# Scan states of an SSM block: float32 products become split float32r products, B·C work moves into the next product block, a modulation row is loaded earlier

## The chip, the cores and the metric

The kernel runs on one core of a Trainium2 chip. The metric is the device time of one execution in microseconds (us), shown as the median of several runs. A core has TensorE (PE, matrix products, with its weight loads shown apart as PEld), VectorE (DVE), ScalarE (ACT), GpSimd (POOL) and SyncE (SP), which here only issues transfers. Each engine works through its own queue in order and waits there for what an instruction needs.

## The reference

All is float32, with a sequence of S = 512 and a width of D = 2048. A first block (Mamba-2 like) is followed by a second one (RG-LRU and attention) whose input is scaled and shifted by a modulation `mod = silu(c) @ w_ada + b_ada`. The change touches the scan of the first block and the loading of c.

```python
proj = rmsnorm(x) @ w_in                       # z, x, B, C, dt
xbc = silu(conv4(x, B, C)); dt = softplus(dt + bias); a = -exp(a_log)
# per chunk of the sequence, 8 groups of 8 heads of 64:
cb = einsum(C, B); y_diag = einsum(cb, decay, x * dt)
y_off = einsum(C, state, exp(cs))
state = state * exp(cs_last) + einsum(B, exp(cs_last - cs), x * dt)
y = rmsnorm((y_diag + y_off + d_skip * x) * silu(z)) @ w_out
```

## The kernel before

Every large float32 product is made of three float32r products ("gemm"): each operand is split into a high half (float32r) and a low half (the rest), and weight-high times act-high, weight-high times act-low and weight-low times act-high are summed (lines 197 to 199). `wchunk` loads 512 KB of weights by SP into one of three `raw` buffers; ScalarE copies each half of it to `hi` (L171) and VectorE subtracts it to get `lo` (L172). `hi` and `lo` have three buffers each, so the split for a later chunk half waits until TensorE has read an earlier one.

The input projection is a loop over 8 groups g. A group is five product blocks of 96 products (16 k-tiles, two column halves, three products): B and C, then for each unit u = 0, 1 (four heads) an x block and a z block. Small steps are placed in a block at a k-tile by `mid[kt]`: `bc_late` (transposes btp of B, products cbp of C and B, the transposed B as btok, the masked cbm) at k-tile 11 of the x block of u = 0; in each z block `ssd_pre` at 11 (transposes tp of x; xdt and xdw, x times dt and times the weight of the state), `ssd_decay` at 12 (four tiles dec per unit, exponentials on ScalarE, then times cbm on VectorE; and cex) and `ssd_states` at 14 (sa, sb: the products of btok and xdw for three chunks; st: the running states). The first unit of the first group has these steps in the next x block. After the z block comes `ssd_unit`: 56 products into yp, chunk 3 first, from dec and xdt (L1186) and from cex and st (L1188). A scheduler writes each engine's order from the program and its priorities; `issue_after` and `high_priority` bind or favour an instruction.

Spread over the groups stand the 96 dot products of `ada` (VectorE, L1214), each on 512 KB of w_ada loaded into one of two buffers. The row c has two halves: when dot product 0 or 48 comes up, its half is loaded (L1205), put through tanh (ScalarE) and finished by two VectorE steps. Dot product 48 falls into group 4, u = 0.

## Time and profile before

| | |
|---|---|
| median of 3 runs | 2068.11 us (2066.47 to 2069.34) |
| profiled execution | 2072.64 us, its span in the trace 2070.9 us |
| PE busy | 2050.8 us (99%), 10032 products |
| PEld busy | 1700.3 us (82%) |
| DVE busy | 1314.9 us (63%) |
| ACT busy | 928.7 us (45%) |
| transfers | 277.26 MB, mean 134 GB/s |
| granted TensorE clock, mean | 0.996 |

The profile shows one execution, which took a little longer than the median of the runs; a sum made from its rows is compared with its own time. Busy time is the union of an engine's instructions. A TensorE row of the timeline says when a product began and how long it was in the engine; products overlap, so the distance of starts is what a product costs in a stream.

### The profile page before, as it was taken

Reading aid. Unit: us, or ns where it says so; the run is one execution under the profiler, and the core shown is the slowest. Engines: PE = TensorE matmul, PEld = TensorE weight load, DVE = VectorE, ACT = ScalarE, POOL = GpSimd, SP = SyncE. Lnnn points to the kernel's source line nnn. Section 1 sums busy time; section 2 is a strip of 40 time slices with the busy share of each in tenths; the row PEclk is TensorE's granted clock in tenths of the full one; section 3 lists DMA queues with packets and bytes.
Section 4 is the critical chain, followed back from the end, with each engine's and each line's share of the span. In section 5 each row is a group of like instructions: output and inputs, shape, how many; then the busy total and the mean of one; then the engine's idle time right before and its main releaser. Section 6 shows DMA issues by size and latency. Waiting matters only on the chain.

```text
span 2070.9 us, 26917 instructions
## 1 busy us (share of the span) xinstructions
PE 2050.8 (99%) x10032; PEld 1700.3 (82%) x10032; DVE 1314.9 (63%) x2308; ACT 928.7 (45%) x1744; POOL 45.4 (2%) x35
## 2 busy tenths in 40 slices
PE   8999999999999999999999999989999999999999
PEld 7888888888878888888788888868888888888887
DVE  6777777687777768777644545476666664764333
ACT  6473444444344443444432433344554554763222
POOL 0000000000000000000000000000000000000000
PEclk9999999999999999999999999989999999999999
DMA  6344555545455454444533332224222223233442
GB/s 227 114 153 159 179 176 187 166 152 182 154 184 170 170 173 147 163 163 135 181 122 128 107 99 95 82 93 159 77 69 67 67 66 105 85 112 106 149 142 92
DMA packets 92627, 277.26 MB, mean 134 GB/s; under 512 B 9744, under 2 KB 19984, under 8 KB 90448
## 3 DMA queue, kind: packets, MB, share of 16 engines
q1 hardware_dynamic: 92208, 275.54, 40.6%
q8 instruction: 78, 1.28, 0.2%
q14 instruction: 53, 0.43, 0.1%
q10 hardware_dynamic: 288, 0.01, 0.0%
HBM read 262.80 MB, written 12.71 MB: 133 GB/s over the span
## 4 chain that ended last, share of the span: by engine, by line
PE 94%; DVE 2%; DMA 1%; ACT 1%; issue 1%; DVEq 0%; ACTq 0%
PE g L197 26%; PE g L198 26%; PE g L199 26%; PE gt L266 1%; PE yp L1186 1%; PE gt L267 1%; PE gt L268 1%; PE yp L1188 1%; DMA adaw<-in_wada 1%; PE op L914 1%; PE g L217 1%; DVE lo L172 1%; PE g L219 1%; PE g L218 1%; PE fm L1060 1%
## 5 line engine op out<-in xcount | busy, mean ns | idle before, releaser
L172 DVE TENSOR_TENSOR lo<-raw,hi 128x512 fp32r<-128x512 f32 (+2 forms) x704 | 476.6, 677 | 544.4 <-ACT hi L171 542.3
L171 ACT ACTIVATE hi<-raw 128x512 fp32r<-128x512 f32 (+2 forms) x704 | 426.8, 607 | 868.6 <-PE g L198 780.8
L197 PE MATMUL g<-hn,hi 128*128 128x512 f32 x1216 | 480.0, 395 | 0.0
L199 PE MATMUL g<-hn,lo 128*128 128x512 f32 x1216 | 474.2, 390 | 0.0
L198 PE MATMUL g<-hn,hi 128*128 128x512 f32 x1216 | 473.9, 390 | 0.0
L197 PEld LDWEIGHTS g<-hn,hi 128*128 128x128 f32 x1216 | 228.3, 188 | 48.8 <-issue 2.4
L199 PEld LDWEIGHTS g<-hn,lo 128*128 128x128 f32 x1216 | 228.2, 188 | 47.8 <-issue 0.2
L198 PEld LDWEIGHTS g<-hn,hi 128*128 128x128 f32 x1216 | 228.4, 188 | 46.7 <-issue 0.2
L198 PE MATMUL g<-h,hi 128*128 128x512 f32 x512 | 200.4, 391 | 1.1 <-DVE h L689 0.8
L197 PE MATMUL g<-ya,hi 128*128 128x512 f32 x512 | 200.2, 391 | 0.0
L199 PE MATMUL g<-ya,lo 128*128 128x512 f32 x512 | 200.2, 391 | 0.0
L198 PE MATMUL g<-ya,hi 128*128 128x512 f32 x512 | 200.0, 391 | 0.0
L199 PE MATMUL g<-h,lo 128*128 128x512 f32 x512 | 199.9, 390 | 0.0
L197 PE MATMUL g<-h,hi 128*128 128x512 f32 x512 | 199.7, 393 | 0.0
L1214 DVE CUSTOM_DVE_ANT_0 adaw<-adaw,adac 128x1024 f32<-128x1024 f32 x96 | 115.6, 1221 | 21.8 <-DMA adaw<-in_wada 21.8
L198 PEld LDWEIGHTS g<-h,hi 128*128 128x128 f32 x512 | 96.2, 188 | 22.5 <-DVE h L689 3.2
L197 PEld LDWEIGHTS g<-ya,hi 128*128 128x128 f32 x512 | 96.5, 188 | 20.4 <-ACT st L1143 0.2
L198 PEld LDWEIGHTS g<-ya,hi 128*128 128x128 f32 x512 | 96.5, 189 | 20.2 <-issue 0.2
L199 PEld LDWEIGHTS g<-ya,lo 128*128 128x128 f32 x512 | 96.4, 188 | 20.3 <-DVE lo L172 0.4
L199 PEld LDWEIGHTS g<-h,lo 128*128 128x128 f32 x512 | 96.1, 188 | 20.3
L197 PEld LDWEIGHTS g<-h,hi 128*128 128x128 f32 x512 | 95.9, 188 | 20.1 <-ACT h L688 1.0
L337 DVE SCALAR_TENSOR_TENSOR xc<-pr,cwh,xc 128x511 f32<-128x511 f32 (+1 forms) x144 | 101.8, 746 | 0.0
(364 smaller groups left out, 2609.9 us busy)
## 6 DMA issues: line engine op xcount, KB each, us to landing
raw<-in_win SPq DMA_DIRECT2D x216, 512.0 KB, 3.5
adaw<-in_wada SPq DMA_DIRECT2D x96, 512.0 KB, 4.7
raw<-in_wout SPq DMA_DIRECT2D x88, 512.0 KB, 3.5
csr<-csd SPq DMA_DIRECT2D x16, 1024.0 KB, 4.8
xT<-in_xT SPq DMA_DIRECT2D x16, 256.0 KB, 4.3
raw<-in_win SPq DMA_DIRECT2D x16, 256.0 KB, 3.2
ydram<-y SPq DMA_DIRECT2D x16, 256.0 KB, 2.1
yst<-ydram SPq DMA_DIRECT2D x8, 512.0 KB, 4.4
```

The lines of the kernel that those rows point to most:

```text
L171: self.last_hi = nc.scalar.activation(hi, raw[:, i * h : i * h + h], AF.Copy).ins
L172: self.last_lo = nc.vector.tensor_tensor(lo, raw[:, i * h : i * h + h], hi.bitcast(F32), ALU.subtract).ins
L197: nc.tensor.matmul(ps[j], hi[:, c], a[:, 0, :], start=kt == 0, stop=False)
L198: nc.tensor.matmul(ps[j], hi[:, c], a[:, 1, :], start=False, stop=False)
L199: mm = nc.tensor.matmul(ps[j], lo[:, c], a[:, 0, :], start=False, stop=kt == nkt - 1)
L217: nc.tensor.matmul(ps[j], hi[:, o], a[:, 0, :], start=first, stop=False)
L218: nc.tensor.matmul(ps[j], hi[:, o], a[:, 1, :], start=False, stop=False)
L219: mm = nc.tensor.matmul(ps[j], lo[:, o], a[:, 0, :], start=False, stop=last)
L266: nc.tensor.matmul(ps[t], a[:, 0, ts], hi, start=k == 0, stop=False)
L267: nc.tensor.matmul(ps[t], a[:, 0, ts], lo, start=False, stop=False)
L337: nc.vector.scalar_tensor_tensor(xc[:, s:], ps[:, : S - s], w(k), xc[:, s:], ALU.mult, ALU.add)
L1214: nc.vector.tensor_tensor_reduce(out=raw, in0=raw, in1=self.cb, op0=ALU.mult, op1=ALU.add, scale=1.0, scalar=0.0, accum_out=self.macc[:, i ...
```

## The change

The state products take split operands: btok and xdw get a high half (ScalarE copy) and a low half (VectorE subtraction), with xw as the unsplit product, and each of the three chunks is three float32r products. The second state is formed straight from the first's PSUM, and the combining steps have high priority. `bc_late` moves to k-tile 11 of the z block of u = 0, ahead of `ssd_pre`, with PSUM tiles from the pool of yp; the steps of u = 1 come one k-tile earlier. The first products of the block that follows a unit are ordered behind the unit's last product (`fence`). The second half of c is loaded when dot product 47 is issued, and its tanh is ordered behind a weight split.

```diff
@@ -142,6 +142,7 @@
     def __init__(self, tc, I, O, dbg):
         self.tc, self.nc, self.I, self.O, self.dbg = tc, tc.nc, I, O, dbg
         self.n = 0
+        self.fence = None
 
     def nm(self, s):
         self.n += 1
@@ -191,13 +192,15 @@
                     after(kt)
                 a = acts[kt]
                 hi, lo = hl[k * 2 // nk]
-                for j in range(ncol):
-                    o = k % (nk // 2) * width + j * P
-                    c = slice(o, o + P)
-                    nc.tensor.matmul(ps[j], hi[:, c], a[:, 0, :], start=kt == 0, stop=False)
-                    nc.tensor.matmul(ps[j], hi[:, c], a[:, 1, :], start=False, stop=False)
-                    mm = nc.tensor.matmul(ps[j], lo[:, c], a[:, 0, :], start=False, stop=kt == nkt - 1)
-                    self.mms.append(mm.ins)
+                with self.tc.issue_after(self.fence) if self.fence is not None and kt == 0 else nullcontext():
+                    for j in range(ncol):
+                        o = k % (nk // 2) * width + j * P
+                        c = slice(o, o + P)
+                        nc.tensor.matmul(ps[j], hi[:, c], a[:, 0, :], start=kt == 0, stop=False)
+                        nc.tensor.matmul(ps[j], hi[:, c], a[:, 1, :], start=False, stop=False)
+                        mm = nc.tensor.matmul(ps[j], lo[:, c], a[:, 0, :], start=False, stop=kt == nkt - 1)
+                        self.mms.append(mm.ins)
+                self.fence = None
                 kt += 1
         assert kt == nkt
         return ps
@@ -507,15 +510,16 @@
             bt = self.conv_silu(ps[0], 32 + g, tmp.tile([P, S], F32, tag="B", name=f"B{g}", bufs=1), prs[0])
             ct = self.conv_silu(ps[1], 40 + g, tmp.tile([P, S], F32, tag="C", name=f"C{g}", bufs=1), prs[1])
             flush()
-            btok = tmp.tile([P, 3, P], F32, tag="btok", name=f"btok{g}", bufs=1)
+            btok = tmp.tile([P, 2, 3, P], F32R, tag="btok", name=f"btok{g}", bufs=1)
             cbm = tmp.tile([P, NC, P], F32, tag="cbm", name=f"cbm{g}", bufs=1)
 
             def bc_late(g=g, bt=bt, ct=ct, btok=btok, cbm=cbm):
-                btp = self.pa.tile([P, NC, P], F32, tag="a", name=f"btp{g}")
+                btp = self.py.tile([P, NC, P], F32, tag="y", name=f"btp{g}")
                 for c in range(3):
                     nc.tensor.transpose(btp[:, c, :], bt[:, c * P : c * P + P], self.ckc("ident"))
-                nc.scalar.activation(btok, btp[:, 0:3, :], AF.Copy)
-                cbp = self.pa.tile([P, NC, P], F32, tag="a", name=f"cbp{g}")
+                nc.scalar.activation(btok[:, 0], btp[:, 0:3, :], AF.Copy)
+                nc.vector.tensor_tensor(btok[:, 1], btp[:, 0:3, :], btok[:, 0].bitcast(F32), ALU.subtract)
+                cbp = self.py.tile([P, NC, P], F32, tag="y", name=f"cbp{g}")
                 for c in range(NC):
                     nc.tensor.matmul(cbp[:, c, :], bt[:, c * P : c * P + P], ct[:, c * P : c * P + P],
                                      start=True, stop=True)
@@ -525,7 +529,6 @@
 
             slow = None
             if g:
-                mid[11] = [bc_late]
                 self.ada(2)
             else:
                 mid[11] = [dt_late]
@@ -552,7 +555,8 @@
                          lambda g=g, u=u, btok=btok, pre=pre: self.ssd_states(g, u, btok, pre)]
                 unit = lambda g=g, u=u, xs=xs, pre=pre, yy=yg: self.ssd_unit(g, u, xs, pre, yy)
                 if g or u:
-                    mid.update({11: steps[0:1], 12: steps[1:2], 14: steps[2:3]})
+                    mid.update({10: steps[0:1], 11: steps[1:2], 13: steps[2:3]} if u else
+                               {11: [bc_late, steps[0]], 12: steps[1:2], 14: steps[2:3]})
                     late.append(unit)
                 else:
                     slow = {1: [bc_late], 5: steps[0:1], 6: steps[1:2], 9: steps[2:3]}
@@ -1108,7 +1112,7 @@
         csr = tmp.tile([P, 4, S], F32, tag="csr", name=self.nm("csr"), bufs=1)
         nc.sync.dma_start(csr, self.csd[h0 : h0 + 4, :].unsqueeze(0).to_broadcast([P, 4, S]))
         xdt = tmp.tile([P, NC, 4, 64], F32, tag="xdt", name=self.nm("xdt"), bufs=1)
-        xdw = tmp.tile([P, 3, 4, 64], F32, tag="xdw", name=self.nm("xdw"), bufs=1)
+        xdw = tmp.tile([P, 2, 3, 4, 64], F32R, tag="xdw", name=self.nm("xdw"), bufs=1)
         for c2 in range(2):
             tp = self.pa.tile([P, 2, 4, 64], F32, tag="a", name=self.nm("tp"))
             for c in range(2):
@@ -1120,9 +1124,12 @@
             nc.vector.tensor_tensor(xdt[:, a:b], tp,
                                     self.dt[:, a:b, h0 : h0 + 4].unsqueeze(3).to_broadcast([P, 2, 4, 64]), ALU.mult)
             b2 = min(b, 3)
-            nc.vector.tensor_tensor(xdw[:, a:b2], tp[:, 0 : b2 - a],
+            xw = tmp.tile([P, 2, 4, 64], F32, tag="xw", name=self.nm("xw"), bufs=1)[:, 0 : b2 - a]
+            nc.vector.tensor_tensor(xw, tp[:, 0 : b2 - a],
                                     self.dtw[:, a:b2, h0 : h0 + 4].unsqueeze(3).to_broadcast([P, b2 - a, 4, 64]),
                                     ALU.mult)
+            nc.scalar.activation(xdw[:, 0, a:b2], xw, AF.Copy)
+            nc.vector.tensor_tensor(xdw[:, 1, a:b2], xw, xdw[:, 0, a:b2].bitcast(F32), ALU.subtract)
         pre.update(csr=csr, xdt=xdt, xdw=xdw)
 
 
@@ -1134,17 +1141,20 @@
         sb = self.pa.tile([P, 1, 4, 64], F32, tag="a", name=self.nm("sb"))
         parts = [sa[:, 0], sa[:, 1], sb[:, 0]]
         for c in range(3):
-            nc.tensor.matmul(parts[c].rearrange("p h d -> p (h d)"), btok[:, c, :],
-                             xdw[:, c].rearrange("p h d -> p (h d)"), start=True, stop=True)
+            o = parts[c].rearrange("p h d -> p (h d)")
+            for i, (a, b) in enumerate(((0, 0), (0, 1), (1, 0))):
+                nc.tensor.matmul(o, btok[:, a, c, :], xdw[:, b, c].rearrange("p h d -> p (h d)"),
+                                 start=i == 0, stop=i == 2)
         st = []
         for c in range(3):
             ns = self.tmp.tile([P, 4, 64], F32, tag="st", name=self.nm("st"), bufs=3)
-            if c == 0:
-                nc.scalar.activation(ns, parts[0], AF.Copy)
-            else:
-                nc.vector.tensor_tensor(
-                    ns, st[-1], self.exl[:, c, h0 : h0 + 4].unsqueeze(2).to_broadcast([P, 4, 64]), ALU.mult)
-                nc.vector.tensor_tensor(ns, ns, parts[c], ALU.add)
+            with self.tc.high_priority():
+                if c == 0:
+                    nc.scalar.activation(ns, parts[0], AF.Copy)
+                else:
+                    nc.vector.tensor_tensor(ns, st[-1] if c > 1 else parts[0],
+                                            self.exl[:, c, h0 : h0 + 4].unsqueeze(2).to_broadcast([P, 4, 64]), ALU.mult)
+                    nc.vector.tensor_tensor(ns, ns, parts[c], ALU.add)
             st.append(ns)
         pre["st"] = st
 
@@ -1187,9 +1197,15 @@
                         else:
                             mm = nc.tensor.matmul(o, st[c - 1][:, h, :], pre["cexs"][c][:, h, :], start=False, stop=True)
                     prev = mm.ins
+        self.fence = prev
         for j in range(2):
             nc.vector.scalar_tensor_tensor(yg[j], xs[j], self.pk("dskip", (g * 4 + u * 2 + j)), yp[j],
                                            ALU.mult, ALU.add)
+
+
+    def ada_c(self, kh):
+        self.cb = self.tmp.tile([P, 1024], F32, tag="adac", name=self.nm("adac"), bufs=1)
+        self.nc.sync.dma_start(self.cb, self.I["cvec"][kh].to_broadcast([P, 1024]))
 
     def ada(self, n):
 
@@ -1200,19 +1216,23 @@
                 return
             self.ada_i += 1
             kh, f = divmod(i, 48)
+            if i == 0:
+                self.ada_c(0)
             if f == 0:
-                cb = self.tmp.tile([P, 1024], F32, tag="adac", name=self.nm("adac"), bufs=1)
-                nc.sync.dma_start(cb, I["cvec"][kh].to_broadcast([P, 1024]))
-                th = self.tmp.tile([P, 1024], F32, tag="adaw", name=self.nm("adat"))
-                nc.scalar.activation(th, cb, AF.Tanh, scale=0.5)
-                nc.vector.scalar_tensor_tensor(cb, th, 1.0, cb, ALU.add, ALU.mult)
-                nc.vector.tensor_scalar(cb, cb, 0.5, None, ALU.mult)
-                self.cb = cb
+                cb = self.cb
+                with self.tc.issue_after(self.last_lo):
+                    th = self.tmp.tile([P, 1024], F32, tag="adaw", name=self.nm("adat"))
+                    nc.scalar.activation(th, cb, AF.Tanh, scale=0.5)
+                    nc.vector.scalar_tensor_tensor(cb, th, 1.0, cb, ALU.add, ALU.mult)
+                    nc.vector.tensor_scalar(cb, cb, 0.5, None, ALU.mult)
             raw = self.tmp.tile([P, 1024], F32, tag="adaw", name=self.nm("adaw"))
             nc.sync.dma_start(raw, I["wada"][kh, f])
             with self.tc.issue_after(self.last_lo):
                 nc.vector.tensor_tensor_reduce(out=raw, in0=raw, in1=self.cb, op0=ALU.mult, op1=ALU.add,
                                                scale=1.0, scalar=0.0, accum_out=self.macc[:, i : i + 1])
+            if i == 47:
+                self.ada_c(1)
+                return
             if i == 95:
                 nc.vector.tensor_tensor(self.mod, self.macc[:, 0:48], self.macc[:, 48:96], ALU.add)
                 nc.vector.tensor_tensor(self.mod, self.mod, self.pk("b_ada", 0, 48), ALU.add)
```

**VectorE, z block of group 3, u = 0, before.** Names carry running numbers: xdt, xdw, st and lo as above, adaw a dot product of `ada`, tp the transposes, g a product block's sums.

```order
L1120 TENSOR_TENSOR xdt_3986<-tp_3995,dt 128x512
L172 TENSOR_TENSOR lo_4158<-raw_4155,hi_4157 128x512
L1123 TENSOR_TENSOR xdw_3987<-tp_3995,dtw 128x256
L1214 ISA adaw_4147,macc<-adaw_4147,adac_1596 128x1024
L1214 ISA macc 128x1
L1214 ISA adaw_4150,macc<-adaw_4150,adac_1596 128x1024
L1214 ISA macc 128x1
L172 TENSOR_TENSOR lo_4162<-raw_4155,hi_4161 128x512
L1145 TENSOR_TENSOR st_4074<-st_4072,exl 128x256
L1147 TENSOR_TENSOR st_4074<-st_4074,sa_4067 128x256
L1145 TENSOR_TENSOR st_4077<-st_4074,exl 128x256
L1147 TENSOR_TENSOR st_4077<-st_4077,sb_4068 128x256
```

The unit's decay products (dec times cbm) are not here: they stand in the x block. **The same place after**, from the two dot products to the first decay product:

```order
L1231 ISA adaw_4232,macc<-adaw_4232,adac_1621 128x1024
L1231 ISA macc 128x1
L1231 ISA adaw_4235,macc<-adaw_4235,adac_1621 128x1024
L1231 ISA macc 128x1
L521 TENSOR_TENSOR btok_3773<-btp_4048,btok_3773 128x384
L526 TENSOR_TENSOR cbm_3774<-cbp_4054,ckt 128x512
L1124 TENSOR_TENSOR xdt_4062<-tp_4064,dt 128x512
L1128 TENSOR_TENSOR xw_4070<-tp_4064,dtw 128x512
L173 TENSOR_TENSOR lo_4246<-raw_4243,hi_4245 128x512
L1124 TENSOR_TENSOR xdt_4062<-tp_4074,dt 128x512
L1132 TENSOR_TENSOR xdw_4063<-xw_4070,xdw_4063 128x512
L1174 TENSOR_TENSOR dec_4100<-dec_4100,cbm_3774 128x512
```

**and on to the last decay product:**

```order
L173 TENSOR_TENSOR lo_4250<-raw_4243,hi_4249 128x512
L1128 TENSOR_TENSOR xw_4080<-tp_4074,dtw 128x256
L1155 TENSOR_TENSOR st_4162<-sa_4149,exl 128x256
L1174 TENSOR_TENSOR dec_4107<-dec_4107,cbm_3774 128x512
L1157 TENSOR_TENSOR st_4162<-st_4162,sa_4149 128x256
L1132 TENSOR_TENSOR xdw_4063<-xw_4080,xdw_4063 128x256
L1155 TENSOR_TENSOR st_4165<-st_4162,exl 128x256
L1174 TENSOR_TENSOR dec_4117<-dec_4117,cbm_3774 128x512
L1157 TENSOR_TENSOR st_4165<-st_4165,sb_4150 128x256
L173 TENSOR_TENSOR lo_4280<-raw_4277,hi_4279 128x512
L1174 TENSOR_TENSOR dec_4127<-dec_4127,cbm_3774 128x512
```

btok's low half and cbm have come in ahead of xdt, xw and the low halves of xdw have been added, and all four decay products now stand here, the last (dec_4127) behind the last state addition and the split lo_4280.

**TensorE, end of the same z block, before:** the last products of the block and the first of the unit.

```order
L197 MATMUL g_3887<-hn_543,hi_4014 128x512
L198 MATMUL g_3887<-hn_543,hi_4014 128x512
L199 MATMUL g_3887<-hn_543,lo_4015 128x512
L1186 MATMUL yp_4092<-dec_4045,xdt_3986 64x128 x2
L1186 MATMUL yp_4093<-dec_4045,xdt_3986 64x128 x2
L1188 MATMUL yp_4092<-cex_4052,st_4077 64x128 x2
L1188 MATMUL yp_4093<-cex_4052,st_4077 64x128 x2
L1186 MATMUL yp_4092<-dec_4035,xdt_3986 64x128 x2
L1186 MATMUL yp_4093<-dec_4035,xdt_3986 64x128 x2
```

**and after:**

```order
L199 MATMUL g_3950<-hn_543,hi_4096 128x512
L1146 MATMUL sb_4150<-xdw_4063,btok_3773 128x256
L200 MATMUL g_3950<-hn_543,hi_4096 128x512
L201 MATMUL g_3950<-hn_543,lo_4097 128x512
L199 MATMUL g_3951<-hn_543,hi_4096 128x512
L200 MATMUL g_3951<-hn_543,hi_4096 128x512
L201 MATMUL g_3951<-hn_543,lo_4097 128x512
L1146 MATMUL sb_4150<-xdw_4063,btok_3773 128x256 x2
L1196 MATMUL yp_4180<-dec_4127,xdt_4062 64x128 x2
L1196 MATMUL yp_4181<-dec_4127,xdt_4062 64x128 x2
L1198 MATMUL yp_4180<-cex_4134,st_4165 64x128 x2
L1198 MATMUL yp_4181<-cex_4134,st_4165 64x128 x2
```

The states' products stood some twelve products earlier in the block before; now the last of them (sb) are directly ahead of the unit, whose first product reads dec_4127.

**TensorE, last unit of the input projection, before:** ya is the operand of the output block, which follows.

```order
L1186 MATMUL yp_8717<-dec_8669,xdt_8610 64x128 x2
L197 MATMUL g_8778<-ya_8782,hi_8798 128x512
L198 MATMUL g_8778<-ya_8782,hi_8798 128x512
L199 MATMUL g_8778<-ya_8782,lo_8799 128x512
L197 MATMUL g_8779<-ya_8782,hi_8798 128x512
L198 MATMUL g_8779<-ya_8782,hi_8798 128x512
L199 MATMUL g_8779<-ya_8782,lo_8799 128x512
L197 MATMUL g_8778<-ya_8785,hi_8798 128x512
L198 MATMUL g_8778<-ya_8785,hi_8798 128x512
L199 MATMUL g_8778<-ya_8785,lo_8799 128x512
L197 MATMUL g_8779<-ya_8785,hi_8798 128x512
L1188 MATMUL yp_8716<-cex_8676,st_8701 64x128 x2
```

**and after:**

```order
L201 MATMUL g_8693<-hn_543,lo_8864 128x512
L1196 MATMUL yp_8910<-dec_8841,xdt_8786 64x128 x2
L1196 MATMUL yp_8911<-dec_8841,xdt_8786 64x128 x2
L1146 MATMUL sb_8874<-xdw_8787,btok_8057 128x256 x3
L1198 MATMUL yp_8910<-cex_8848,st_8889 64x128 x2
L1198 MATMUL yp_8911<-cex_8848,st_8889 64x128 x2
L1196 MATMUL yp_8910<-dec_8831,xdt_8786 64x128 x2
L1196 MATMUL yp_8911<-dec_8831,xdt_8786 64x128 x2
L1198 MATMUL yp_8910<-cex_8838,st_8886 64x128 x2
```

The ten products of the output block that stood between the two parts of chunk 3 now follow the unit, and the states' last products (sb) stand in their place.

## Rows read from the trace of the kernel before

**Rows 1.** The page's busy times: engine, us, share of the span, instructions.

```profile
PE 2050.8 (99%) x10032; PEld 1700.3 (82%) x10032; DVE 1314.9 (63%) x2308; ACT 928.7 (45%) x1744; POOL 45.4 (2%) x35
```

**Rows 2.** The page's chain that ended last, share of the span by engine.

```profile
PE 94%; DVE 2%; DMA 1%; ACT 1%; issue 1%; DVEq 0%; ACTq 0%
```

**Rows 3.** Waits, 100 to 1000 us, PE: total us, times, longest.

```profile
PE yp L1188 <- DVE st L1147: 3.2, 2, 1.6
```

**Rows 4.** Timeline of PE, z block, group 3, u=0: start, us, engine, line, operation.

```profile
439.63 0.39 PE L197 MATMUL g<-hn,hi 128*128 128x512 f32 x1
...
446.20 0.39 PE L199 MATMUL g<-hn,lo 128*128 128x512 f32 x1
446.44 1.03 PE L1117 MATMUL tp<-ckt,xs 128*128 128x128 f32 x8
...
451.43 1.03 PE L1137 MATMUL sa<-xdw,btok 128*128 128x256 f32 x4
452.29 0.59 PE L1137 MATMUL sb<-xdw,btok 128*128 128x256 f32 x2
...
452.95 0.40 PE L198 MATMUL g<-hn,hi 128*128 128x512 f32 x1
...
455.58 0.66 PE L1186 MATMUL yp<-dec,xdt 128*64 128x128 f32 x8
456.17 0.66 PE L1188 MATMUL yp<-cex,st 128*64 128x128 f32 x8
```

**Rows 5.** Timeline of PE around bc_late, group 3, x block.

```profile
423.42 0.49 PE L516 MATMUL btp<-ckt,B 128*128 128x128 f32 x3
423.74 1.06 PE L520 MATMUL cbp<-C,B 128*128 128x128 f32 x8
...
424.87 0.39 PE L198 MATMUL g<-hn,hi 128*128 128x512 f32 x1
```

**Rows 6.** Timeline of PE in the second block, 384-wide float32r products.

```profile
1475.14 0.34 PE L267 MATMUL gt<-lo,qn 128*128 128x384 f32 x1
1475.31 0.34 PE L268 MATMUL gt<-hi,qn 128*128 128x384 f32 x1
```

**Rows 7.** Timeline of DVE, z block, group 3, u=0.

```profile
446.32 1.22 DVE L1214 CUSTOM_DVE_ANT_0 adaw<-adaw,adac 128x1024 f32<-128x1024 f32 x1
...
447.46 0.69 DVE L1120 TENSOR_TENSOR xdt<-tp,dt 128x512 f32<-128x512 f32 x1
448.06 0.68 DVE L1123 TENSOR_TENSOR xdw<-tp,dtw 128x512 f32<-128x512 f32 x1
...
449.94 0.42 DVE L1123 TENSOR_TENSOR xdw<-tp,dtw 128x256 f32<-128x256 f32 x1
450.28 1.22 DVE L1214 CUSTOM_DVE_ANT_0 adaw<-adaw,adac 128x1024 f32<-128x1024 f32 x1
...
455.69 0.42 DVE L1147 TENSOR_TENSOR st<-st,sb 128x256 f32<-128x256 f32 x1
```

**Rows 8.** Lines by form, DVE: busy us, mean ns, idle before, releaser.

```profile
L172 DVE TENSOR_TENSOR lo<-raw,hi 128x384 fp32r<-128x384 f32 x16 | 8.9, 557 | 15.4 <-ACT hi L171 14.9
```

**Rows 9.** Timeline of SP's queue and PE, group 4, u=0; brackets: idle before, releaser.

```profile
569.34 0.33 SPq L1205 DMA_DIRECT2D adac<-in_cvec  x1
...
581.44 0.66 PE L1188 MATMUL yp<-cex,st 128*64 128x128 f32 x8 [1.60 <-DVE st L1147]
```

**Rows 10.** Timeline of PE, last unit.

```profile
999.21 0.66 PE L1188 MATMUL yp<-cex,st 128*64 128x128 f32 x8 [1.65 <-DVE st L1147]
```

**Rows 11.** Timeline of ACT and PE, first unit.

```profile
112.96 0.63 ACT L1163 ACTIVATE dec<-dec 128x512 f32<-128x512 f32 x1
114.53 0.66 PE L1186 MATMUL yp<-dec,xdt 128*64 128x128 f32 x8
```

**Rows 12.** Windows: length, busy us of PE, PEld, DVE, ACT, POOL, clock, DMA share, GB/s.

```profile
580.00:582.00 2.00, 0.56 (x10) 0.56 (x12) 2.00 (x6) 1.79 (x5) 0.00 (x0) 1.00 0.94 381
1356.00:1358.00 2.00, 1.21 (x6) 1.21 (x6) 0.07 (x1) 1.24 (x2) 0.00 (x0) 0.57 0.45 180
```

## The prediction

> **What bounds the kernel now.** I read the busy times first: TensorE is busy for 99% of the span and VectorE for 63% [rows 1]. Then the chain of work that ended last: 94% of it is TensorE, 2% VectorE [rows 2]. So a saving counts only if TensorE issues less or waits less, and a loss arises wherever TensorE is made to wait. Then the waits of the first 1000 us, where the changed code runs: TensorE's only listed waits there are two, 3.2 us together, both on the last state addition [rows 3]. The kernel thus has almost no waiting to give back, and the question is whether the new order adds some. For that I read the timeline of one z product block (group 3, first unit, u=0) on TensorE and VectorE [rows 4, 7], and the first, the ninth and the last unit apart [rows 9 to 11].
>
> **Prices.** A 512-wide float32r product is issued every (446.20 − 439.63)/29 = 0.2266 us, over 30 in a row [rows 4]. A 384-wide one takes 1475.31 − 1475.14 = 0.17 us [rows 6]. No 256-wide float32r product is in the trace. A line through both widths gives 0.12 us, which I take; the bounds are half of a 512-wide one, 0.113, and no gain at all under 384, 0.173. On VectorE, from start to start: 512 wide 448.06 − 447.46 = 0.60 us, 256 wide 450.28 − 449.94 = 0.34, one w_ada dot product 447.46 − 446.32 = 1.14 [rows 7]. The 384-wide low half of B's transposes: its like has 0.557 us of busy time [rows 8], less the 0.08 by which a 512-wide record (0.68) outlasts its step, 0.48.
>
> **The state products.** Before, three float32 products of 256 columns (six records) stand between 451.43 and 452.95, with one 0.2266 product among them [rows 4]: 1.29 us a unit. After, nine at 0.12: 1.08. That is −0.21 a unit, between −0.27 and +0.27 by the bounds. TensorE is the bound, so this counts wherever no new wait follows: at the seven u=1 units, −1.5 us.
>
> **Unit u=0 of groups 1, 2, 3, 5, 6, 7.** Here bc_late (transposes of B, C B products, 1.22 us on TensorE: 424.87 − 423.42 less one 0.2266 product [rows 5]) moves from the x block into the z block ahead of the turning of x. Moved with it on VectorE is the mask product cbm, and therefore everything that reads cbm: the four decay products, which used to be done under the x block's products, well ahead of the unit. The unit's first product (yp, chunk 3) reads the last of these four. I count from T0, the start of bc_late's first transpose, which stands where the first transpose of x stood (446.44).
>
> TensorE comes to yp at: 1.22 for bc_late, 451.43 − 446.44 = 4.99 for transposes and 18 products, 1.08 for the states, and 455.58 less (452.95 − 0.2266) = 2.86 for the last 12 products [rows 4]. Together T0 + 10.15. Before it was 1.22 (spent earlier) + 455.58 − 446.44 = 9.14, + 0.1 for the small wait at 456.17 (eight such products take some 0.49): 10.46.
>
> The last decay product comes by two counts. First, VectorE's queue, which starts at 446.32, T0 − 0.12 [rows 7]: in its new order stand ahead of and including that product two dot products, one 384-wide, twelve 512-wide and six 256-wide steps: 2.28 + 0.48 + 7.20 + 2.04 = 12.0. With the 0.08 of the record's tail and 0.06 to TensorE (addition ends 456.11, yp 456.17 [rows 4, 7]) it is seen at T0 + 12.0. Second, a chain that no faster queue shortens: the order puts the addition of the third state and one weight split ahead of it. The third state's last product starts 0.12 before yp's place, 10.03, and lasts at most 0.34 [rows 6]; then addition 0.34, split 0.60, decay product 0.68, 0.06: T0 + 12.05. Both say 12.0. TensorE waits 12.0 − 10.15 = 1.9 us, and since the next block's first products are now held behind the unit's last (the fence), nothing fills it. Net 12.0 − 10.46 = +1.55 a unit, six units: **+9.3**. Queued behind the late decay product are the z block's gate steps, which TensorE doesn't need soon. The dot products' transfers are not late here: there are two ahead of the unit where there were three, and the buffers of both come free in the x block.
>
> [...]
>
> [...]
>
> **Unit u=0 of group 4.** Its order has one dot product and the last decay product ahead of the last addition, with no split before it: 12.0 − 1.14 − 0.60 = 10.3, next to no wait. Before, this unit waited 1.60 us for the c row: its transfer was issued at 569.34 and yp could go on at 581.44 [rows 9]. That row is now issued a block ahead. −1.6 − 0.21 = **−1.8**. If the tanh and its two VectorE steps (about 1.7 us) came back in another wait, it would be 0; the order places them in the u=1 blocks, behind that unit's decay products.
>
> **First unit.** Before, nine products of the next block (2.04 us) went ahead of yp, which waited for ScalarE's decay chain (its last exponential at 112.96, yp at 114.53 [rows 11]). They now stand behind. The chain itself starts no earlier. **+2.0**, bounds 0 (the chain gets in sooner) and 3.3 (the 1.2 us of bc_late ahead of the transfer it needs too).
>
> **Last unit.** Before, ten products of the output block (2.27 us) went between the two halves of yp's chunk 3, and still TensorE waited 1.65 us on the state addition [rows 10]. Now none fills it. **+2.2**, bounds 0 and 5, the latter if the high-priority additions queue behind the splits of the output block's operands too.
>
> The start-up's first c row is held behind a weight split now; its first reader stands far behind on VectorE, 0.
>
> **Sum.** 9.3 − 1.8 − 1.5 + 2.0 + 2.2 = +10.2 us. The profiled execution took 2072.64 (span 2070.9 and 1.7 around it), so 2082.8 under the profiler; the median of the runs is 2068.11, 4.5 below, so **2078.3** for the runs.
>
> **Rivals.**
> *VectorE keeps up (faster).* If the last decay product were there by T0 + 10.15 at all six units, each would gain 0.31, −1.9; with the ends costing nothing as well it is −1.9 − 1.8 − 1.5 = −5.2, 2062.9. VectorE must be 1.9 us earlier than both counts. For: it is busy 63% overall and idle ahead of 446.32. Against: the chain through the third state starts on TensorE itself. It decides only if the order's split and addition cost under 0.1 us together. Chance 0.07.
> *Half a loss (same).* If the six waits are 1.0 instead of 1.9 (+0.65 each, 3.9) and the ends cost 1 us in all, it is 3.9 − 1.8 − 1.5 + 1 = +1.6, 2069.7. For: ends and latencies are each uncertain by some tenths. Chance 0.13.
> *Narrow products cost as 384-wide ones (0.173).* Then states are 1.56: +0.48 on each of the 14 units, +6.7, 2085. For: nine products bring nine weight loads of full width, whatever their columns. Against: the 384-wide step is under the 512-wide one. Chance 0.10.
> *The clock falls in the new gaps.* One stretch of TensorE work with gaps, 1356 to 1358, has granted clock 0.57, while 580 to 582, with a gap of 1.6 us, kept 1.00 [rows 12]. [...] The second row has just such a gap as I forecast, which speaks against it. Chance 0.06.
> *My forecast*, 2073 to 2084: 0.64.
>
> **The numbers.** 0.2% is 4.1 us, about what a measurement of this kernel can tell from no change. Faster 0.07; same 0.13; slower 0.64 + 0.10 + 0.06 = 0.80. The range goes from 2068 (most of the half loss) to 2088 (both costly rivals, or the last unit's upper bound).
>
> **What the profile after would show.** Right: at six places, one a group with groups 0 and 4 left out, TensorE waits 1.5 to 2.2 us at yp's dec product for VectorE's dec, together 9 to 12 us, the largest new line of the waits. State products 0.11 to 0.13 apart. The wait for the c row is gone. The chain of work gains VectorE's share. Wrong: yp's first product follows at once there (then the queue was shorter than I count), the wait names the state or ScalarE, state products stand 0.17 apart, or the granted clock falls behind the gaps. The forecast is most easily wrong by the length of the wait, which counts six times, and by the two ends.

## The result and the profile after

The changed kernel takes 2089.33 us (median of 5 executions, 2085.07 to 2091.96) against 2068.6 of the kernel before in the same session (2068.11 was known when the forecast was made): a ratio of 1.0094, interval 1.0082 to 1.0107. That is 20.7 us slower, where 10 were forecast, and just above the range, which ended at 2088. The traced execution was the fastest of the five, 2085.07 us.

The page's busy times of the changed kernel (answering to [rows 1]):

```profile
span 2083.3 us, 27074 instructions
...
PE 2047.4 (98%) x10080; PEld 1699.2 (82%) x10080; DVE 1331.8 (64%) x2348; ACT 944.0 (45%) x1776; POOL 47.9 (2%) x35
```

TensorE is busy for slightly less time than before (2050.8), while the span is 12.4 us longer: the time has gone into waits. TensorE's waits of the changed kernel, 100 to 1020 us (columns: total, times, longest), answering to [rows 3]:

```profile
PE yp L1196 <- DVE dec L1174: 14.3, 7, 3.3
PE sb L1146 <- ACT xdw L1131: 2.9, 3, 1.5
PE yp L1198 <- DVE st L1157: 0.5, 1, 0.5
```

The first line is the forecast wait, seven times: once 3.3 us at the first unit and six times 1.83. The same z block as in [rows 4, 7], group 3, u=0, on TensorE after the change:

```profile
452.09 0.49 PE L519 MATMUL btp<-ckt,B 128*128 128x128 f32 x3
...
458.66 0.75 PE L1146 MATMUL sa<-xdw,btok 128*128 128x256 f32 x5
459.25 0.40 PE L200 MATMUL g<-hn,hi 128*128 128x512 f32 x1
...
461.92 0.40 PE L1146 MATMUL sb<-xdw,btok 128*128 128x256 f32 x2
464.15 0.66 PE L1196 MATMUL yp<-dec,xdt 128*64 128x128 f32 x8 [1.83 <-DVE dec L1174]
```

and on VectorE:

```profile
452.03 1.22 DVE L1231 CUSTOM_DVE_ANT_0 adaw<-adaw,adac 128x1024 f32<-128x1024 f32 x1
...
455.39 0.68 DVE L1124 TENSOR_TENSOR xdt<-tp,dt 128x512 f32<-128x512 f32 x1
455.99 0.68 DVE L1128 TENSOR_TENSOR xw<-tp,dtw 128x512 f32<-128x512 f32 x1
...
462.48 0.41 DVE L1157 TENSOR_TENSOR st<-st,sb 128x256 f32<-128x256 f32 x1
462.81 0.68 DVE L173 TENSOR_TENSOR lo<-raw,hi 128x512 fp32r<-128x512 f32 x1
463.41 0.68 DVE L1174 TENSOR_TENSOR dec<-dec,cbm 128x512 f32<-128x512 f32 x1
```

T0 is 452.09 here. The first dot product starts at T0 − 0.06, VectorE then works without a gap through the 21 steps that the forecast counted, and TensorE gets its decay product at 464.15, T0 + 12.06 (forecast 12.0). Five state products take 459.25 − 458.66 = 0.59 us, 0.118 each (forecast 0.12). The trace bears out the line through the widths of [rows 4, 6]. On VectorE the 512-wide step from xdt to xw is 455.99 − 455.39 = 0.60 us, as in [rows 7].

### The profile page after: what moved, and what is told of

It reads as the page before. It is cut to its first block, busy times and chain, and to the rows that moved or that the text cites. A ratio compares the mean times of both kernels' runs of the same rounds, so it can differ in the third digit from the quotient of the medians.

```text
span 2083.3 us, 27074 instructions
## 1 busy us (share of the span) xinstructions
PE 2047.4 (98%) x10080; PEld 1699.2 (82%) x10080; DVE 1331.8 (64%) x2348; ACT 944.0 (45%) x1776; POOL 47.9 (2%) x35
## 4 chain that ended last, share of the span: by engine, by line
PE 68%; DVE 2%; DMA 1%; ACT 0%; issue 0%; DVEq 0%; ACTq 0%
PE g L200 19%; PE g L199 19%; PE g L201 19%; PE gt L269 1%; PE gt L270 1%; PE gt L271 1%; PE op L918 1%; PE yp L1196 1%; PE fm L1064 1%; PE yp L1198 1%; PE sp L880 0%; PE sp L881 0%; PE sp L879 0%; DVE lo L173 0%; PE sp L902 0%
## 5 line engine op out<-in xcount | busy, mean ns | idle before, releaser
L340 DVE SCALAR_TENSOR_TENSOR xc<-pr,cwh,xc 128x511 f32<-128x511 f32 (+2 forms) x144 | 101.4, 744 | 0.0
```

What stands on the lines that cost most here:

```text
L340: nc.vector.scalar_tensor_tensor(xc[:, s:], ps[:, : S - s], w(k), xc[:, s:], ALU.mult, ALU.add)
```

## The experiments

Theories when the first four kernels ran. *G*: waits and lost fills (products of the next block that used to run during a wait) cost 12 to 13 us, and the rest, about 8, is TensorE's lower clock behind the new gaps, in some executions at some of them. *W*: the waits alone, the clock has no part.

**no_fence**, the fence undone:

```diff
-        self.fence = prev
```

> Only the fence is undone: products of the next block may go ahead of the unit again (the order has nine or ten, 2.0 to 2.3 us, between the last state product and the unit at u=0). Theory G (waits plus clock: the changed kernel loses 12 to 13 us to TensorE waits and lost fills, and the rest, about 8 us, to stretches of 3.4 us at the lower TensorE clock that follow such gaps in some executions, 1.7 us each): no wait and no gap, so the time falls to 2067 (2064 to 2070), the runs lie within 4 us again, and the mean granted clock is 0.996 or more in all. Theory W (waits alone, the clock is no part of it): only the waits are given back, six of 1.83, 1.9 at the first unit, 2.2 at the last, so 2089.3 - 15.1 = 2074.

Measured 2070.31 (11 executions, 2068.9 to 2072.65; ratio 1.0006, interval 0.9997 to 1.0014), not told from the kernel before. All of the loss but 1 us hangs on the fence. TensorE ahead of the same unit in this kernel:

```profile
454.13 0.40 PE L1146 MATMUL sb<-xdw,btok 128*128 128x256 f32 x2
454.37 0.39 PE L199 MATMUL g<-hn,hi 128*128 128x512 f32 x1
...
456.41 0.39 PE L199 MATMUL g<-hn,hi 128*128 128x512 f32 x1
456.73 0.66 PE L1196 MATMUL yp<-dec,xdt 128*64 128x128 f32 x8
```

Ten products of the next block stand between the last state product and the unit. On VectorE the decay product is as late as in the changed kernel (it starts at 455.61, 11.3 us after this block's first transpose of B, as there), but TensorE doesn't notice: its listed waits, 2.9 us together, are for xdw and lo. W's 2074 is out; G's 2067 is 3 us too low and its range just missed, so the rest of the change gains nothing.

**fill**, unused products in the waits:

```diff
+            self.hn0 = hn[0]
...
+        if u == 0 and g != 4:
+            w = self.hn0[:, 0, 0:P]
+            for i in range(8 if g else 14):
+                with tc.issue_after(prev if prev is not None else self.mms[-1]):
+                    prev = nc.tensor.matmul(yp[i % 2], w, self.hn0[:, 0, :], start=True, stop=True).ins
```

> The changed kernel with extra products that nobody uses: eight 512-wide products (1.81 us) ahead of the unit u=0 of groups 1, 2, 3, 5, 6, 7 and fourteen (3.17 us) ahead of the first, into the unit's own PSUM tiles, which it overwrites. TensorE is busy through the waits, and the units start no earlier. Theory G: no time is given back by itself, but the lower clock does not follow the gaps: 2081 (2078 to 2084), runs within 4 us, clock 0.996 or more. Theory W: unchanged, 2089 with runs from 2085 to 2092.

Measured 2083.86 (2082.84 to 2085.28; ratio 1.0071, interval 1.0059 to 1.0084): 5.5 us less than the changed kernel, with more work, and a group still takes 123.3 us in its trace, as in the first trace of the changed kernel: the units' own products start no earlier. Only the gaps are gone, seven of them; the shorter ones of group 4 and of the last unit (1.3 to 1.5 us) are left, and in this trace the granted clock is 1.00 at 114 to 118 and at 340 to 344 us and 0.998 in the mean; the five executions have mean clocks of 0.996 to 0.998. What keeping TensorE busy gives back is the part that is not waiting: 5.5 us (5.0 against after_2 below), with G's 2081 (2078 to 2084) and not W's 2089. The size is rough, since there are five executions here: the intervals of the two ratios overlap a little, though nine of the changed kernel's ten executions are longer than all five of these. The other 14.5 over the kernel before are waits and lost fills.

**after_2**, the changed kernel again:

> The changed kernel once more, for a second trace of it and more executions, since the first traced one was its fastest. Theory G (the rest beyond waits and lost fills is the lower TensorE clock after the new gaps): 2089 (2085 to 2093), mean granted clock from 0.993 to 0.997, and the time of an execution rises by about 2 us for each 0.001 that its clock is lower; a trace with a clock under 0.996 shows the unit of some 1.83 us wait at the lower clock. Rival R (the first session's executions were disturbed): 2082 to 2085 now, like its first trace.

Measured 2088.88 (2087.09 to 2089.99; ratio 1.009, interval 1.0076 to 1.0104). The changed kernel's ten executions, the first five and these, by time with their mean granted clock:

```
2085.07 0.997   2085.94 0.996   2087.09 0.996   2087.31 0.996   2088.88 0.995
2089.33 0.994   2089.93 0.994   2089.99 0.995   2090.03 0.995   2091.96 0.993
```

G's time and its clock range hold, and rival R (disturbed executions, 2082 to 2085) is out. The second trace, at 0.995, shows where the clock fell. Windows of it (length, busy us of PE, PEld, DVE, ACT, POOL, granted clock, DMA share, GB/s):

```profile
115.00:119.00 4.00, 3.83 (x36) 3.83 (x38) 4.00 (x7) 1.08 (x3) 0.00 (x0) 0.50 0.55 229
342.00:346.00 4.00, 3.59 (x38) 3.59 (x40) 3.90 (x7) 2.79 (x8) 0.00 (x0) 0.61 0.01 3
465.00:469.00 4.00, 2.16 (x34) 1.91 (x34) 4.00 (x8) 1.55 (x4) 0.00 (x0) 1.00 0.21 87
589.00:593.00 4.00, 4.00 (x16) 3.01 (x16) 3.01 (x7) 0.32 (x1) 0.00 (x0) 0.62 0.43 131
```

The first, second and fourth begin about where TensorE goes on after a wait, the third holds one and what follows it. In the first the clock is 0.50 for the whole stretch, after the first unit's wait; in the second its mean is 0.61, in the third 1.00, although both units had waited the same 1.83 us; the fourth, at 0.62, follows the wait of 1.83 us of a state product in group 4. What the second cost is seen in the timeline of its unit against the third's:

```profile
342.41 0.76 PE L1196 MATMUL yp<-dec,xdt 128*64 128x128 f32 x8 [1.83 <-DVE dec L1174]
342.95 1.07 PE L1198 MATMUL yp<-cex,st 128*64 128x128 f32 x8
...
346.75 0.61 PE L1196 MATMUL yp<-dec,xdt 128*64 128x128 f32 x8
...
467.38 0.66 PE L1196 MATMUL yp<-dec,xdt 128*64 128x128 f32 x8 [1.84 <-DVE dec L1174]
467.87 0.61 PE L1198 MATMUL yp<-cex,st 128*64 128x128 f32 x8
...
470.05 0.61 PE L1196 MATMUL yp<-dec,xdt 128*64 128x128 f32 x8
```

346.75 − 342.41 = 4.34 us against 2.67: 1.67 us for one fall of the clock. A fall can cost more. From the first unit's first product to the second unit's it is 145.19 − 115.17 = 30.02 us in this trace, 143.62 − 114.85 = 28.77 in the first trace and 141.95 − 114.78 = 27.17 in fill's, where the clock is 1.00 at 114 to 118 us: 2.85 and 1.60 us. In the first trace of the changed kernel, of all these gaps, it fell at the first unit's alone (114 to 118 us: 0.59; by single us from 114 to 119: 0.86, 0.50, 0.50, 0.50, 0.94, together some 3.4 us at 0.50), and at none of the six, each followed by 4 us at 1.00.

**fence_only**, the kernel before with the fence's lines:

> The kernel before with the fence alone. Its fills, 9 products ahead of the first unit, 7 in the unit u=0 of group 4, 10 in the last, go behind the units: 2.0 + 1.6 + 2.3 = 5.9 us. Theory G: in addition the clock falls at some of these three gaps (3.6, 3.2 and 3.9 us long then), 1.7 us each: 2069 + 5.9 + 3 to 5 = 2079 (2076 to 2082). Theory W (no clock): 2075. Rival: the fence costs nothing where no decay product is late, 2069.

Measured 2077.61 (2076.43 to 2081.91; ratio 1.004, interval 1.0027 to 1.0054): 8.5 us for an edit that adds no work. Its waits, 100 to 1020 us, and the windows behind the three longest:

```profile
PE yp L1191 <- DVE st L1150: 8.0, 4, 3.9
PE yp L1189 <- DVE dec L1167: 2.0, 1, 2.0
...
113.00:117.00 4.00, 3.25 (x32) 3.25 (x34) 3.96 (x7) 1.83 (x3) 0.00 (x0) 0.61 0.78 231
584.00:588.00 4.00, 3.18 (x30) 3.19 (x32) 3.80 (x7) 3.97 (x12) 0.00 (x0) 0.61 0.28 115
1005.00:1009.00 4.00, 3.45 (x32) 3.45 (x34) 2.68 (x6) 2.34 (x4) 0.00 (x0) 0.50 0.42 159
```

The waits that the products of the next block had covered are 10.0 us now, where [rows 3] had 3.2, and at all three gaps of 2 to 3.9 us the clock fell in this trace (0.61, 0.61 and 0.50 over 4 us), which is the slowest of the five executions (2081.91, clock 0.994; the others have 0.996 and 0.997). "Costs nothing" is out. G's 2079 fits; W's 2075 lies at the low end of what the ratio's interval allows, so that it is the clock in the trace which speaks against W here, and not the median.

**bc_back**, the move of bc_late alone undone (its PSUM pool goes back too, not shown):

```diff
-                               {11: [bc_late, steps[0]], 12: steps[1:2], 14: steps[2:3]})
+                               {11: steps[0:1], 12: steps[1:2], 14: steps[2:3]})
...
+                mid[11] = [bc_late]
```

> Only the place of bc_late is undone (back in the x block, PSUM tiles from the first pool); fence, float32r states and the early row stay. The decay products are early again, so no wait at the six units; the first and the last unit keep theirs. Theory G: the six units give back 9.3 and the clock most of its 8 us: 2073 (2070 to 2076). Theory W: 2089.3 - 9.3 = 2080.

Measured 2081.14 (2078.73 to 2083.24; ratio 1.006, interval 1.0046 to 1.0074). Both expectations missed their reason. The wait at the decay product is gone, but another took its place, at the states:

```profile
PE yp L1199 <- DVE st L1158: 7.2, 8, 1.0
PE yp L1197 <- DVE dec L1175: 2.6, 1, 2.6
...
```

Seven units u=0 and the last wait up to 1.0 us for the last state addition: with split operands VectorE has two more steps ahead of the states, and with the decay products gone from here the order puts dot products there (one starts at 454.37 and one at 457.22, the addition at 460.50). The fence leaves that wait bare too.

This trace also shows that the length of a gap alone doesn't decide about the clock. Windows behind the first unit's wait of 2.58 us, and at the last unit, where waits of 1.45 and 0.51 us come close together:

```profile
114.00:118.00 4.00, 3.58 (x58) 3.37 (x59) 4.00 (x7) 0.31 (x1) 0.00 (x0) 1.00 0.75 236
1004.00:1008.00 4.00, 3.49 (x35) 3.48 (x36) 2.41 (x6) 1.95 (x4) 0.00 (x0) 0.57 0.83 250
```

Behind the longer wait the clock stayed at 1.00, and behind the shorter ones it was 0.57.

**bc_back_no_fence**, both undone:

> Both undone, so what is left of the change are the float32r state products, the early row and u=1's steps one k-tile earlier. Both theories: no new wait; the states give back 0.21 us in 16 units, 3.4, and the row 1.6, against 2068.6 of before: 2063.6. If the narrow products cost as much as 384-wide ones, or the operands' splits delay TensorE elsewhere: 2067 to 2070.

Measured 2074.54 (2073.26 to 2076.65; ratio 1.0027, interval 1.0017 to 1.0038), 11 us above what was expected. The remaining edits don't gain; in this combination they lose 5. Its trace is 7.0 us longer than before_2's (below), and 3.4 of them are there by the start of the second unit (142.06 against 138.63): u=1's first state products wait 1.75 us in all for their operands (up to 133.97, 134.69 and 136.08), and the clock falls there (0.57 at 136 to 140 us). The rest isn't taken apart, and its cause stays open.

**states_only** (before with the split state products and the priority of their combining) and **pre_only** (before with the early row):

> The kernel before with the split float32r state products (and the high priority of their combining) alone. Theory S (bc_back_no_fence was 5 us slower because the split operands make the states late: the 128x512 and 128x256 low halves stand between x's turning and the state products on VectorE): 2075 (2072 to 2078). Rival P (the products' saving of 0.21 us in 16 units counts, and that run's loss came from u=1's steps being one k-tile earlier): 2066.

> The kernel before with the early c row alone. The wait of 1.60 us in group 4 goes: 2069.3 - 1.6 = 2067.7 (2067 to 2069). Rival: the row's tanh and two VectorE steps come back as a wait in u=1 of group 4, or the wait is taken up by the products that filled it: 2069.3.

Measured 2071.15 (ratio 1.0006, interval 0.9998 to 1.0015) and 2070.16 (1.0007, 0.9997 to 1.0016): neither is told from no change. So theory S was too dark and P too bright, and pre_only's 2067.7 missed while its rival, no change, held. Why the states save nothing is seen at u=1 of group 3 in the changed kernel, where no decay product is late:

```profile
510.78 0.39 PE L199 MATMUL g<-hn,hi 128*128 128x512 f32 x1
511.40 0.39 PE L1146 MATMUL sb<-xdw,btok 128*128 128x256 f32 x1 [0.23 <-ACT xdw L1131]
```

511.40 − 510.78 is 0.62 where a product's step is 0.23: the third state's operand comes late. Its high half is a ScalarE copy (510.94) queued behind a weight copy (510.41) that waits for TensorE (0.65 us). 0.4 us of waiting eats the 0.21 that the products save. And the row: in pre_only (SP's queue, and ScalarE)

```profile
568.14 0.33 SPq L1196 DMA_DIRECT2D adac<-in_cvec  x1
...
574.17 1.06 ACT L1213 ACTIVATE adat<-adac 128x1024 f32<-128x1024 f32 x1 [4.31 <-DMA adac<-in_cvec]
```

its transfer is issued 1.20 us before the one of [rows 9], and the whole trace is 1.28 us earlier there (unit 7, counted from 0, starts at 503.68 against 504.96). Its one buffer still holds the first half until dot product 47 has read it (VectorE, 566.88 to 568.03), so an issue that is earlier in the program waits for the same thing.

**pre_two**, the row with two buffers and its transfer eight dot products ahead, and **best**, that with u=1's steps one k-tile earlier (pre_two shown against pre_only, in part):

```diff
-        self.cb = self.tmp.tile([P, 1024], F32, tag="adac", name=self.nm("adac"), bufs=1)
+        self.cb = self.tmp.tile([P, 1024], F32, tag="adac", name=self.nm("adac"), bufs=2)
...
+            if i == 40:
+                cb0 = self.cb
+                self.ada_c(1)
+                self.cn, self.cb = self.cb, cb0
```

> The kernel before with the early c row alone, but with two buffers for it and the transfer's issue eight dot products ahead. Theory B (in the changed kernel and in pre_only the transfer still starts only when dot product 47 has read the only buffer, at 568.14 in pre_only's trace, so the row is not early at all): the tanh no longer waits, the unit's wait of 1.6 to 1.9 us goes, 2069.1 - 1.6 = 2067.5 (2066 to 2068.5). Rival: the wait comes from the tanh and the two VectorE steps standing in the queues, not from the transfer: 2069.

> As pre_two, and u=1's steps one k-tile earlier, as in the changed kernel; no fence, float32 states, bc_late in the x block. Expected: as pre_two, and of the last unit's wait of 1.65 us up to 1 us less: 2066.5 (2065 to 2068). Rival: the last state addition stands behind other work whatever the k-tile: as pre_two.

Measured 2067.21 (ratio 0.9992, interval 0.9984 to 1.0001) and 2067.53 (0.9989, 0.998 to 0.9998) against 2069.37. TensorE's waits of pre_two, 100 to 1020 us, no longer have the one in group 4:

```profile
PE yp L1188 <- DVE st L1147: 1.3, 1, 1.3
PE g L199 <- DVE lo L172: 0.2, 1, 0.2
```

So the buffer was the reason. The gain, about 2 us, is the size of the wait; pre_two's interval just touches no change, best's just doesn't, and the two aren't told apart. In best's trace the last unit waits 0.7 us instead of 1.3, but 1.1 us of waits for xdw have come in. By the medians they are the fastest versions of the study.

**short_dots**, the changed kernel with 18 dot products cut to 64 columns (the modulation lacks the rest):

```diff
+                    self.short = u == 0 and g != 4
                     self.ada(3)
+                    self.short = False
...
+                w = 64 if self.short else 1024
```

> The changed kernel with 18 of the 96 dot products over 64 columns instead of 1024 (the modulation lacks the rest): those of which two each stand ahead of the unit u=0 in groups 1, 2, 3, 5, 6, 7. The order then has the last decay product ahead of the last state addition. Theory Q (VectorE's queue with the dot products makes the decay products late): no wait at the six units, 11 us and the clock falls after them given back, the fence's loss at both ends stays: 2074.5 (2072 to 2078). Rival (the split states are late as in bc_back, a wait of 1.0 us at each unit): 2081.

Measured 2076.24 (2072.11 to 2077.75; ratio 1.0032, interval 1.0021 to 1.0042), 13 us less than the changed kernel. Its waits, 100 to 1020 us:

```profile
PE yp L1199 <- DVE dec L1177: 3.4, 1, 3.4
PE sb L1149 <- ACT xdw L1134: 3.2, 3, 1.6
...
PE yp L1201 <- DVE st L1160: 0.5, 1, 0.5
```

The six waits are gone and the first unit's stays. Theory Q holds; the rival's wait at the states isn't there. The cut also changed the order (last decay product ahead of the last addition), so the queue's length and that order aren't separated.

**before_2**, the kernel before again:

> The kernel before once more, for a second trace: the first traced execution, 2072.64 us, was slower than every other of its program then. Theory G: that trace holds more of the lower clock than usual, so this one is 2067 to 2070 with a clock of 0.997 or 0.998, and until 1340 us both traces agree within 2 us and show no lower clock.

One execution, 2067.52, clock 0.998, span 2065.7. The first trace of before, 5.2 us longer, was an unlucky one. It was 2.1 us later by the start of unit 14, counted from 0 (944.81 against 942.69), a little more than expected, and lost the rest from there to 1365 us, in a longer wait of the last unit (1.65 us against before_2's 1.08) and at the lower clock of [rows 12] (0.50 at 1360 to 1364 us, 0.85 in before_2). This trace is the one to compare with below.

## Why the prediction was wrong

Direction, place and the mechanism of the waits were right, and the largest term to within a few per cent. The number was too low by 11 us: some 5.5 of them are the clock, some 4 the smaller terms of the sum, and 1.2 the base.

**The step that failed: the clock.** The prediction gave "The clock falls in the new gaps" a chance of 0.06 and left it out of the sum, arguing from [rows 12] that a gap of 1.6 us had kept 1.00 once. One gap says little about an event that comes in some executions. The changed kernel's two traces have nine and ten gaps of 1.2 to 3.4 us; the first has a fall at one of them (0.59), after_2's at three (0.50, 0.61 and 0.62), 1.6 to 2.9 us each where it was read off. fill shows the sum, some −5 us on the median, by keeping TensorE busy through seven of the gaps while the units start no earlier. The upper end of the range counts a price for this rival that no row of before shows; what the traces showed is a fall at none or one of the six units and another at the first unit, 1.67 us at the one and 1.60 and 2.85 us at the first.

**Terms of the sum,** from the traces after and fill against before_2, in stretches where the clock stayed up (in after 1.00 from 340 to 710 and from 955 to 1364 us), but for the second block, where it falls too (0.50 at 1356 to 1360 us in before_2, at 1368 to 1376 in after) (distances between first or last products of units, which are counted from 0: unit 6 is u=0 of group 3):

| term | forecast | measured | how |
|---|---|---|---|
| six units u=0 | +9.3 | +9.1 | start of unit 5 to unit 6: 73.90 against 72.38, 1.52 each |
| u=1 | −1.5 | +0.7 | start of unit 4 to unit 5: 49.40 against 49.30, 0.1 at seven |
| group 4, u=0 | −1.8 | −0.5 | start of unit 6 to unit 10: 246.40 against 245.14, less 1.52 and twice 0.1 |
| first unit | +2.0 | +3.3 | end of unit 1: fill 145.23, before_2 141.91 (the two traces of before differ by 1.3 here) |
| last unit | +2.2 | +0.5 to +1.7 | end of unit 14 to the second block's first sums: 407.56 (after), 408.78 (after_2), 407.06 (before_2; the first trace of before has 408.34, so this row is rough) |
| second block | 0 | +0.7 | from there to the end: fill 713.35, before_2 712.67 |
| sum | +10.2 | about +14.5 | fill's median less before's: +14.5 |

- *Six units.* Both counts, the queue and the chain through the third state, said 12.0; it is 12.06. short_dots shows that without most of the two dot products the wait goes altogether, so the second count was not a floor: it held only for the order in which the last addition stands ahead. "Nothing fills it" was right and weighed more than I gave it: no_fence shows that the late decay products alone cost nothing.
- *States.* The product's price was right (0.118; the line gives 0.12 with 0.173 for the 384-wide step and 0.113 with the 0.17 of [rows 6]), its value wrong: the prediction took it that at u=1 "no new wait follows", and a ScalarE copy queued behind a weight copy made one.
- *Group 4.* "That row is now issued a block ahead" is the step that failed in this term. I read the program's order and not what the transfer waits for, its single buffer. In the changed kernel the tanh still waits for the row and holds xdw's high half behind it, which is the 1.17 us (1.83 in after_2) at the state product there.
- *First and last unit.* At the upper bound and within the bounds. fence_only shows these two and group 4 by themselves, 8.5 us with the clock.
- *The base.* The forecast is in effect the median of three executions, 2068.11, plus the sum. The 4.5 us by which the traced execution stood above it were the lower clock and a slow stretch of that one execution (mean clock 0.996, before_2's 0.998). In the later sessions the kernel before has medians of 2069.13 to 2069.37, up to 1.3 us more than the base.

What stays open: why after_2's gap of 1.83 us at 342 us is followed by the lower clock (0.61) and the like one at 467 us is not (1.00), why bc_back's 2.58 us was not (1.00), and the 0.7 us in the second block. There the kernels wait for a VectorE step that before_2 has in time (0.83 us at 1439 us in the first trace); every trace with split state products has that wait, 0.59 to 1.76 us, states_only too (1.52), and of the others pre_two alone, with 0.3. Why is not shown.

## What to carry to other kernels

An ordering edge that holds back independent work costs what that work used to cover: 8.5 us by itself here, and about 20 together with late operands that without it cost nothing that could be measured. It turned waits that the next block's products had covered into gaps, and behind some of them the granted clock fell as well (0.50 to 0.62 over 4 us). Before counting on a transfer that is issued earlier in the program, look for what frees its buffer. And price a gap on a busy TensorE as its length plus some chance of a fall of the clock, 1.6 to 2.9 us here, not its length alone.

## What the runs showed of the hardware

A wait of TensorE of 1.83 us was followed by a granted clock of 0.61 over 4 us at one unit of after_2 (and of 0.62 behind a state product) and by 1.00 at another unit of the same execution, at 1.67 us for the unit's fall; in the first trace of the changed kernel all six such waits were followed by 1.00; in fence_only's trace all three gaps of 2.0 to 3.9 us were followed by 0.50 to 0.61, and bc_back's of 2.58 us by 1.00. Filling gaps with products whose result nobody reads made the kernel some 5 us faster (5.5 and 5.0). Narrow float32r products went at 0.118 us for 256 columns against 0.2266 for 512, 0.52 of it.
